# Two hybrid layers on one core: forget gates ahead of the queries, more low parts on GpSimd, other places for small steps

## The chip, the cores and the metric

The kernel runs on one core of a Trainium2 chip. The metric is the device time of one execution in microseconds (us); less is better. A core has five engines with a queue each: TensorE (PE; PEld is its weight load), VectorE (DVE), ScalarE (ACT), GpSimd (POOL) and SyncE (SP), which issues most transfers. PSUM is the memory that TensorE writes to, SBUF the memory for all else.

## The reference

A trunk of two layers over 512 tokens, with 16 meta tokens ahead of them (T = 528), width 1024, in float32. Each layer:

```python
xn = rmsnorm(h, attn_norm_g)
proj = xn @ w_in                       # fq, fk, fv, flog, rq, rk, rv, rg
logf = log_sigmoid(flog + b_fgate)     # 8 forget gates; c = cumsum(logf)
# 8 attention heads of 64: softmax(q.k / 8 + c[t] - c[s]) v, causal
# 4 retention heads of 128: rotary q and k, decay gamma_h^(t-s), chunks of 128
ret = head_groupnorm(ret) * silu(rg)
h = h + concat(fox_out, ret) @ w_out
hn = rmsnorm(h, ffn_norm_g)
h = h + (silu(hn @ w_gate) * (hn @ w_up)) @ w_down      # inner width 2816
```

At the end stands one more rmsnorm, and the 16 meta tokens are dropped.

## The kernel before, in words

Everything is held transposed: 128 channels on the partitions, the 528 tokens along the columns. A float32 product is made of three: each operand is split into a high part (hi) and the rest (lo), and hi x hi, w-hi x x-lo and w-lo x x-hi are summed in PSUM. So one *step* of a projection (one block of 128 x 128 weights) is six matmuls in layer 0, where the columns are cut in two halves of 264, and three where only the 512 real tokens are wanted (parts of layer 1). A *job* of `dense_steps` is eight steps with one weight tile `raw` of 128 x 1024. Its high part `whi` is cast by ScalarE (L199) and its low part `wlo` is subtracted (L202) by VectorE in pieces of 128 x 512 or, where the job's argument `pool` is set, by GpSimd in pieces of 128 x 128. `whi` and `wlo` have two buffers each; the next job's tile is converted at steps 1 and 4 of the job before.

PSUM is cut into two tiles of two banks (`psd`, results of the projections) and four of one bank (`psa`, all else), which go round in the order in which TensorE's steps ask for them.

The order on TensorE is written out by hand: a list `plan` of steps, into which `spread` and `ret_places` place the small steps (scores, transposes, sums of a norm) by their number among the steps of the projections. The order on the other engines is made by a scheduler from the same program; what stands in a `tc.high_priority()` block goes first, and what is pinned keeps its place.

What the change touches:
- `forget_sums`: the eight forget gates. z is scaled by the norm's R (L403), |z + b|, exp, ln on ScalarE, min(z + b, 0) (L407), a subtraction (L408) and a running sum (L409), then split into `fs` (L411, L412).
- `q_done`, `k_done`: the queries' and keys' projection leaves PSUM as `tq` (L442, L456), is split into `qo`/`qs` and `kc`/`kx`, and the forget sums are put below the keys in `kc` (L467). The first score (L519) reads `kc`.
- `out_proj` (`w_out`) and the first three gate and up blocks of `ffn` (plain blocks): which engine makes their low parts.
- The head norm of the retention: `col_rstd` lets TensorE sum the squares (L298, into psa), ScalarE take Ln (L303) and Exp (L304), and VectorE refine and scale (`nwt` L305, L307, L308, then `d` L792). `d` times the gate `sg` (silu, L418) is split into `mxh` and `mxl`, which the last steps of the output projection multiply. `ret_places(hd, ...)` sets the places of these steps; the ninth number is the head norm's.
- The tail: for the last token columns the squares of eight blocks are added by VectorE into `acc`, and the last ones summed apart on TensorE (L1164).

An `ACT_TABLE_LOAD` stands wherever ScalarE goes over from one family of functions to another, as between Exp and silu.

Of the kernel before, what the change touches and what calls it, by code (L numbers as in the profile page):

```python
# [39 lines left out]
def hybrid_kernel(ctx, tc, x_t, w_in, w_fl, w_out, w_gate, w_up, w_down, vecs, b_fg, rope, decay, mask, ident, out_t):  # L40
# [11 lines left out]

    idt = const.tile([128, 128], F32, name="idt")
    msk = const.tile([128, T], F32, name="msk")
    nc.vector.memset(msk[:, 0:T - 128], 0.0)
    pick = const.tile([32 + FH, FH], F32, name="pick")
    vec = const.tile([128, vecs.shape[1]], F32, name="vec")
    nc.scalar.dma_start(vec, vecs)
# [6 lines left out]
    nc.vector.memset(epsc, EPS)  # L65
    onec = const.tile([128, 1], F32, name="onec")
    nc.vector.memset(onec, 1.0)

    p_tiles, t_tiles, pm_tiles, v_tiles, end_tiles, q_tiles, k_tiles, f_tiles = [], [], [], [], [], [], [], []
    rot = {"pm": 0}  # L70
# [328 lines left out]
    def forget_sums(l, st):  # L399
        z = st["z"]  # L400
        z2 = tt("z2")[0:FH]
        with ExitStack() if l else tc.high_priority():
            nc.vector.scalar_tensor_tensor(z, z, RSC, st["R"][0:FH, :], ALU.mult, ALU.mult)  # L403
            nc.scalar.activation(z2, z, AF.Abs, bias=bfg[:, l:l + 1])
            nc.scalar.activation(z2, z2, AF.Exp, scale=-1.0)
            nc.scalar.activation(z2, z2, AF.Ln, bias=onec[0:FH])
        nc.vector.tensor_scalar(z, z, bfg[:, l:l + 1], 0.0, ALU.add, ALU.min)  # L407
        nc.vector.tensor_sub(z, z2, z)  # L408
        nc.vector.tensor_tensor_scan(z2, z, z, 0.0, ALU.add, ALU.max)  # L409
        with ExitStack() if l else tc.high_priority():  # L410
            nc.scalar.copy(f_tiles[0][0:FH], z2)  # L411
            nc.vector.tensor_sub(f_tiles[0][32:32 + FH], z2, f_tiles[0][0:FH].bitcast(F32))  # L412

# [19 lines left out]
    def fox_dense(l, g, ly, real, st):  # L433

        QC = REAL if real else FULL
        first = l + g == 0


        def q_done(ps):
            tq = tt("tq")  # L440
            with tc.high_priority() if first else ExitStack():
                nc.vector.scalar_tensor_tensor(sv(tq, real), pv(ps, real), RSC / 8.0, sv(ly["R"], real), ALU.mult, ALU.mult)  # L442
            st["q"] = []
            for s in range(2):
                t = at(f"qs{s}")
                a0, a1 = ROWS[s]
                b0, b1 = ROWS[1 - s]
                for o in (q_tiles[s], t):
                    nc.scalar.copy(sv(o, real, a0, a1), sv(tq, real, a0, a1))
                nc.vector.tensor_sub(sv(t, real, b0, b1), sv(tq, real, a0, a1), sv(q_tiles[s], real, a0, a1).bitcast(F32))  # L450
                st["q"].append((q_tiles[s], t))


        def k_done(ps):
            tk = tt("tq")
            nc.vector.scalar_tensor_tensor(sv(tk, False), pv(ps, False), RSC, sv(ly["R"], False), ALU.mult, ALU.mult)  # L456
            st["k"] = []
            for s in range(2):
                kc = k_tiles[s]
                kx = at(f"kx{s}")  # L460
                a0, a1 = ROWS[s]
                b0, b1 = ROWS[1 - s]
                nc.scalar.copy(kc[a0:a1, :], tk[a0:a1, :])
                nc.scalar.copy(kx[b0:b1, :], tk[a0:a1, :])
                nc.vector.tensor_sub(kx[a0:a1, :], tk[a0:a1, :], kc[a0:a1, :].bitcast(F32))
                hd = 2 * g + s
                (nc.gpsimd if g else nc.vector).tensor_scalar(kc[b0:b0 + 32 + FH, :], f_tiles[0].bitcast(F32), pick[:, hd:hd + 1], 0.0, ALU.mult, ALU.add)  # L467
                st["k"].append((kc, kx))

        def v_done(ps):  # L470
            vt = v_tiles[0]
            for t, (c0, c1) in zip(ps, FULL):
                nc.vector.scalar_tensor_tensor(vt[:, c0:c1], t[:, 0:c1 - c0], RSC, ly["R"][:, c0:c1],
                                               ALU.mult, ALU.mult)
            repeat(vt, SEQ, 1, SEQ + 32)
            if not real:
                repeat(vt, 0, 2, SEQ + 64)
            st["vt"] = vt

# [333 lines left out]
    def out_proj(l, rnd, mix, real):  # L813

        cols = REAL if real else FULL
        xs = lambda k: mix[k]["mix"]
        return sum([dense_steps(w_out[l, rnd, m2], [(4 * s, xs, 4, cols, add_h(2 * m2 + s, real)) for s in range(2)],
                                rnd == 0 or m2 < 2, rnd == 1 and m2 == 1) for m2 in range(NK // 2)], [])

    def ffn(l, st, real, last):  # L820
        QC = REAL if real else FULL
# [234 lines left out]
        for r, (f0, f1) in enumerate(ROUNDS):  # L1056
            for f in range(f0, f1):
                if f < PLAIN:
                    steps += dense_steps(w_gate[l, f], [(0, xs, NK, QC, g_done(f) if f else held.append)], banks=f == 1)
                    steps += dense_steps(w_up[l, f], [(0, xs, NK, QC, u_done(f))])  # L1060
                    continue
                u = Unit(f)
                steps += u.head()
                for v in tails:
                    v.last()
                    steps += v.tail()
                tails = []
                u.rest()
                steps += u.middle()
                if fills:  # L1070
                    p, g0, g1 = fills.pop(0)
                    j = down_job(p, g0, g1)
                    steps += down(j, 0, 2 * p, g0, g1, not real)
                    u.last()
                    steps += u.tail()
                    steps += down(j, 1, 2 * p + 1, g0, g1, False)
                else:
                    tails = [u]
            for p, g0, g1 in fills:
# [10 lines left out]
        else:  # L1090
# [34 lines left out]
            def square_b(m):  # L1125
                if m == 0:
                    t = fft("S", F32, (128, 6, w), 2)
                    fin["one"] = [t[:, i, 0:nb] for i in range(3)]
                    fin["acc"], fin["rb"], fin["tb"] = (t[:, i, 0:nb] for i in range(3, 6))
                    d = fin["acc"]  # L1130
                elif m < NK - 3:
                    fin["sq", m] = d = tt("sq")[:, 0:nb]
                else:
                    d = fin["one"][m - NK + 3]
                pin(nc.scalar.activation(d, h[m][:, cb], AF.Square))

            def sum_b(m):
# [78 lines left out]

            def after_7():
                square_b(7)
                v = psum_a()[:, 0:nb]
                sums(v, [fin["one"][0], fin["acc"]] + fin["one"][1:])  # L1220
                out_a(2)
                out_a(4)
                out_a(6)
                scale_b(3)
                root(fin["rb"], v)
                scale_b(4, 5, 6, 7)
                for i in range(3):
# [18 lines left out]
    def layer(l):  # L1246
# [66 lines left out]
        sums = [lambda: forget_sums(l, ly)]  # L1313
        plan = [lambda: enter_att(l), start]
        if l == 0:
            plan += [lambda: squares(ly, FULL, True, False)] + qk[:-2] + [first_parts] + gates + qk[-2:] + stats + [lambda: ly["wait"].pop(0)()] + sums + [lambda: ly["wait"].pop(0)()]
        else:
            plan += [lambda: squares(ly, FULL)] + q[:7] + stats + q[7:] + gates + sums + k
        plan += v + [ropes]
# [5 lines left out]

        for g in range(2):
            main, rest = fs[g]
            m0, r0, places = (((7 if l else 10.5, 31 if l else 32.5), (34, 40.5), (13, 33.5, 35.5, 37.5, 39, 40.5, 43, 44, 47.5, 48)),
                              ((0.5, 31.5), (32, 40), (13, 33.5, 35.5, 39.5, 39, 41.5, 43, 44, 47.5, 48)))[g]
            plan += merge(rd(g, "vqkg") + sum(fd(g + 1), []),  # L1330
                          spread(main, *m0), spread(rest, *r0), ret_places(g, *places))
# [6 lines left out]
        op = out_proj(l, 1, mixes[1], real)  # L1338
        base += op[0:3] + op[4:7] + op[8:11] + op[12:15]
        plan += merge(base, spread(main, 2, 46.5), spread(rest, 51, 56),  # L1340
                      ret_places(2, 26, 23.5, 24.5, 32, 28, 33.5, 36, 56.5, 40.5, 57.5),
                      ret_places(3, 52, 45.5, 47.5, 57.5, 55.5, 58.5, 60, 64.1, 63, 64.2))
        plan += [op[3], op[7], op[11], op[15]] + op[16:]
        up = ffn(l, ff, real, real)
        plan += [lambda: enter("ffn"), start_ffn] + up
# [78 lines left out]
```

## Time and profile before

| | before |
|---|---|
| median of three runs | 1271.29 us |
| the three runs | 1271.49, 1268.26, 1271.29 us |
| profiled execution | 1268.53 us, span 1266.7 us |
| TensorE busy | 1251.2 us (99%) |
| VectorE busy | 991.9 us (78%) |
| ScalarE busy | 704.8 us (56%) |
| GpSimd busy | 273.3 us (22%) |
| mean granted clock of TensorE | 0.997 |

The profile is of one execution; times in it count from the start of its span. A row of the timeline has the start, the duration, the engine, the line of the kernel, the operation, the tile written and the tiles read, the count, and in brackets how long the engine had been idle and who released it. Rows with a count above one give the time from the first start to the last end. Line numbers are those of the kernel before; after the change they move by a few (L442 becomes L440, L519 L524, L418 L416).

### The profile page before, as it was taken

To read this page: it belongs to the slowest core of one execution; us is meant where nothing else is said; L and a number is where in the kernel's file an instruction comes from. 1 tells how busy PE (TensorE), PEld (TensorE's weight loads), DVE (VectorE), ACT (ScalarE), POOL (GpSimd) and SP (SyncE) were. 2 spreads that over 40 slices of the span, in tenths; PEclk is the share of its full clock that TensorE was granted. 3 is DMA by queue.
4 is the path that set the end of the run, shared out by engine and by line. 5 is a ranking of instruction groups with operands and counts; after the bars stand their busy time and mean duration, and the time that the engine had idled before them with its cause. 6 is when DMAs were issued, how large, how long until landed. Compare 5 with 4: busy or idle time off the path is not lost.

```text
span 1266.7 us, 23526 instructions
## 1 busy us (share of the span) xinstructions
PE 1251.2 (99%) x9225; PEld 1194.1 (94%) x9225; DVE 991.9 (78%) x1804; ACT 704.8 (56%) x1301; POOL 273.3 (22%) x539
## 2 busy tenths in 40 slices
PE   9999999999999999999999999999999999999997
PEld 8899999999999999999999989998789999999996
DVE  8887756779988888887786877567899888888867
ACT  6766655676444444444466766557764444444445
POOL 3455546420000000000126556554100000000000
PEclk9999999999999999999999999999999999999999
DMA  6122222223333333332322122222223333333321
GB/s 218 50 76 75 76 77 72 72 67 118 104 97 100 100 101 100 101 101 84 101 77 84 60 86 74 70 90 67 100 94 123 100 101 101 100 101 101 100 84 67
DMA packets 43342, 116.19 MB, mean 92 GB/s; under 512 B 5088, under 2 KB 12000, under 8 KB 43232
## 3 DMA queue, kind: packets, MB, share of 16 engines
q1 hardware_dynamic: 42800, 114.41, 28.1%
q8 instruction: 72, 1.18, 0.4%
q14 instruction: 38, 0.31, 0.1%
q10 hardware_dynamic: 432, 0.29, 0.1%
HBM read 112.58 MB, written 2.10 MB: 91 GB/s over the span
## 4 chain that ended last, share of the span: by engine, by line
PE 93%; ACT 3%; DVE 3%; issue 1%; DMA 0%; ACTq 0%; DVEq 0%
PE psd L225 30%; PE psa L907 18%; PE psd L1042 14%; PE psd L907 13%; PE psa L225 5%; PE psa L1042 4%; PE psa L429 2%; PE psa L519 2%; PE psa L589 1%; PE psa L756 1%; PE psa L722 1%; ACT whi L199 1%; PE psa L298 0%; ACT xh L327 0%; DMA raw<-w_in 0%
## 5 line engine op out<-in xcount | busy, mean ns | idle before, releaser
L202 POOL TENSOR_TENSOR wlo<-raw,whi 128x128 fp32r<-128x128 f32 x504 | 258.2, 548 | 260.1 <-ACT whi L199 259.7
L225 PE MATMUL psd<-xh,whi 128*128 128x264 f32 (+1 forms) x792 | 195.5, 314 | 0.2 <-DVE tq L442 0.2
L225 PE MATMUL psd<-xl,whi 128*128 128x264 f32 (+1 forms) x792 | 186.7, 303 | 0.6 <-DVE xl L328 0.6
L225 PE MATMUL psd<-xh,wlo 128*128 128x264 f32 (+1 forms) x792 | 187.0, 304 | 0.0
L225 PEld LDWEIGHTS psd<-xh,whi 128*128 128x128 f32 x792 | 128.6, 189 | 5.0 <-issue 0.6
L225 PEld LDWEIGHTS psd<-xh,wlo 128*128 128x128 f32 x792 | 127.2, 188 | 6.2 <-DVE wlo L202 0.4
L225 PEld LDWEIGHTS psd<-xl,whi 128*128 128x128 f32 x792 | 127.8, 189 | 5.4 <-DVE xl L328 1.4
L199 ACT CAST whi<-raw 128x512 fp32r<-128x512 f32 (+1 forms) x168 | 97.9, 613 | 41.5 <-PE psd L225 28.4
L895 ACT CAST whi<-raw 128x1024 fp32r<-128x1024 f32 (+2 forms) x62 | 54.9, 885 | 51.3 <-PE psd L907 39.8
L895 ACT CAST fwhi<-raw 128x1024 fp32r<-128x1024 f32 (+2 forms) x62 | 55.6, 897 | 47.5 <-PE psd L907 40.0
L122 POOL MEMSET kc<- 64x528 f32 x2 | 1.1, 533 | 345.4 <-PE psa L907 345.4
L896 DVE TENSOR_TENSOR wlo<-raw,whi 128x1024 fp32r<-128x1024 f32 (+2 forms) x62 | 62.9, 1014 | 12.7 <-ACT whi L895 12.6
L896 DVE TENSOR_TENSOR fwlo<-raw,fwhi 128x1024 fp32r<-128x1024 f32 (+2 forms) x62 | 64.0, 1032 | 11.1 <-ACT fwhi L895 10.9
L907 PE MATMUL psa<-th,whi 128*128 128x264 f32 (+1 forms) x232 | 65.4, 282 | 0.0
L907 PE MATMUL psa<-th,wlo 128*128 128x264 f32 (+1 forms) x232 | 65.4, 282 | 0.0
L907 PE MATMUL psa<-tl,whi 128*128 128x264 f32 (+1 forms) x232 | 65.3, 282 | 0.0
L907 PE MATMUL psa<-th,fwhi 128*128 128x264 f32 (+1 forms) x224 | 63.4, 283 | 0.0
L907 PE MATMUL psa<-tl,fwhi 128*128 128x264 f32 (+1 forms) x224 | 63.3, 283 | 0.0
L907 PE MATMUL psa<-th,fwlo 128*128 128x264 f32 (+1 forms) x224 | 63.2, 282 | 0.0
L536 ACT ACTIVATE pr<-pr,nmax 128x144 f32<-128x144 f32 (+1 forms) x64 | 36.8, 576 | 45.4 <-DVE nmax L523 26.1
L895 ACT CAST fwhi<-S 128x1024 fp32r<-128x1024 f32 x20 | 21.0, 1049 | 68.6 <-PE psa L907 66.5
L973 ACT COPY e<-psa 128x264 f32<-128x264 f32 (+1 forms) x114 | 42.8, 376 | 28.4 <-PE psa L907 24.1
(365 smaller groups left out, 4041.2 us busy)
## 6 DMA issues: line engine op xcount, KB each, us to landing
raw<-w_in SPq DMA_DIRECT2D x54, 512.0 KB, 3.5
raw<-w_gate SPq DMA_DIRECT2D x44, 512.0 KB, 3.9
fraw<-w_up SPq DMA_DIRECT2D x38, 512.0 KB, 3.5
raw<-w_down SPq DMA_DIRECT2D x64, 256.0 KB, 2.9
raw<-w_out SPq DMA_DIRECT2D x16, 512.0 KB, 3.4
raw<-w_down SPq DMA_DIRECT2D x32, 192.0 KB, 2.5
raw<-w_up SPq DMA_DIRECT2D x6, 512.0 KB, 3.5
h<-x_t SPq DMA_DIRECT2D x8, 264.0 KB, 4.5
```

The source lines that it names most:

```text
L199: pin(nc.scalar.copy(hi, job["raw"][:, c0:c1]), pinned)
L202: pin(sub(lo[:, c:c + step], job["raw"][:, c0 + c:c0 + c + step], hi[:, c:c + step].bitcast(F32)), pinned)
L225: nc.tensor.matmul(ps[1][b][:, 0:c1 - c0], w[:, wk, :], x[:, c0:c1], start=(k == 0 and i == 0), stop=(k == n - 1 and i == 2))
L429: nc.tensor.transpose(ps[:, 128 * j:128 * j + 128], src[:, o:o + 128], idt)
L519: nc.tensor.matmul(sc[0:nq, 0:c1 - c0], qq[:, q0:q0 + nq], kk[:, c0:c1], start=(i == 0), stop=(i == 1))
L536: nc.scalar.activation(pr, pr, AF.Exp, bias=nmax[0:nq], scale=-1.0, accum_out=rsum)
L589: nc.tensor.matmul(po[:, c0:SEQ], v[:, j, :], pp[:, j, META + c0:T], start=(j == 0 and i == 0), stop=(j == 4))
L895: nc.scalar.copy(hi, src)
L896: nc.vector.tensor_sub(lo, src, hi.bitcast(F32))
L907: nc.tensor.matmul(bank()[:, 0:b.shape[-1]], a[:, o + k, :], b, start=(fresh and k == 0 and i == 0), stop=(k == n - 1 and i == 2), skip_gr ...
L973: nc.scalar.copy(self.t["e"][:, i], self.t["x"][:, 0:w])
L1042: nc.tensor.matmul(v[:, 0:c1 - c0], a[:, s * n + k, :], b[:, c0:c1], start=(k == 0 and i == 0), stop=(k == n - 1 and i == 2))
```

## The change

`forget_sums` runs whole at high priority in layer 0, and all of it stands ahead of the queries in the plan; the subtraction is done in the running sum. In the first pair of heads the second `kc` goes to ScalarE, the first stays on VectorE at high priority. The first clearing of `msk` goes to GpSimd. GpSimd makes the low parts of all jobs of `out_proj` and of the plain gate and up blocks. In the tail two squares instead of three are kept apart. Places move: head 0 of the retention 10.5 to 11 and 37.5 to 38, head 2's norm 40.5 to 49, head 3's 60 to 60.6 and 63 to 63.6.

```diff
-    nc.vector.memset(msk[:, 0:T - 128], 0.0)
...
+    nc.gpsimd.memset(msk[:, 0:T - 128], 0.0)
...
             nc.scalar.activation(z2, z2, AF.Ln, bias=onec[0:FH])
-        nc.vector.tensor_scalar(z, z, bfg[:, l:l + 1], 0.0, ALU.add, ALU.min)
-        nc.vector.tensor_sub(z, z2, z)
-        nc.vector.tensor_tensor_scan(z2, z, z, 0.0, ALU.add, ALU.max)
-        with ExitStack() if l else tc.high_priority():
+            nc.vector.tensor_scalar(z, z, bfg[:, l:l + 1], 0.0, ALU.add, ALU.min)
+            nc.vector.tensor_tensor_scan(z2, z2, z, 0.0, ALU.add, ALU.subtract)
             nc.scalar.copy(f_tiles[0][0:FH], z2)
             nc.vector.tensor_sub(f_tiles[0][32:32 + FH], z2, f_tiles[0][0:FH].bitcast(F32))
...
-                (nc.gpsimd if g else nc.vector).tensor_scalar(kc[b0:b0 + 32 + FH, :], f_tiles[0].bitcast(F32), pick[:, hd:hd + 1], 0.0, ALU.mult, ALU.add)
+                own, of = kc[b0:b0 + 32 + FH, :], f_tiles[0].bitcast(F32)
+                if g:
+                    nc.gpsimd.tensor_scalar(own, of, pick[:, hd:hd + 1], 0.0, ALU.mult, ALU.add)
+                elif s:
+                    nc.scalar.activation(own, of, AF.Copy, scale=pick[:, hd:hd + 1])
+                else:
+                    with tc.high_priority():
+                        nc.vector.tensor_scalar(own, of, pick[:, hd:hd + 1], 0.0, ALU.mult, ALU.add)
...
         return sum([dense_steps(w_out[l, rnd, m2], [(4 * s, xs, 4, cols, add_h(2 * m2 + s, real)) for s in range(2)],
-                                rnd == 0 or m2 < 2, rnd == 1 and m2 == 1) for m2 in range(NK // 2)], [])
+                                True, rnd == 1 and m2 == 1) for m2 in range(NK // 2)], [])
...
-                    steps += dense_steps(w_gate[l, f], [(0, xs, NK, QC, g_done(f) if f else held.append)], banks=f == 1)
-                    steps += dense_steps(w_up[l, f], [(0, xs, NK, QC, u_done(f))])
+                    steps += dense_steps(w_gate[l, f], [(0, xs, NK, QC, g_done(f) if f else held.append)], True, banks=f == 1)
+                    steps += dense_steps(w_up[l, f], [(0, xs, NK, QC, u_done(f))], True)
...
             def after_7():
                 square_b(7)
+                sum_b(5)
                 v = psum_a()[:, 0:nb]
-                sums(v, [fin["one"][0], fin["acc"]] + fin["one"][1:])
+                sums(v, [fin["one"][0], fin["acc"], fin["one"][1]])
...
-            plan += [lambda: squares(ly, FULL, True, False)] + qk[:-2] + [first_parts] + gates + qk[-2:] + stats + [lambda: ly["wait"].pop(0)()] + sums + [lambda: ly["wait"].pop(0)()]
+            plan += [lambda: squares(ly, FULL, True, False)] + qk[:-2] + [first_parts] + gates + qk[-2:] + stats + sums + [lambda: ly["wait"].pop(0)()] * 2
...
-                      ret_places(2, 26, 23.5, 24.5, 32, 28, 33.5, 36, 56.5, 40.5, 57.5),
-                      ret_places(3, 52, 45.5, 47.5, 57.5, 55.5, 58.5, 60, 64.1, 63, 64.2))
+                      ret_places(2, 26, 23.5, 24.5, 32, 28, 33.5, 36, 56.5, 49, 57.5),
+                      ret_places(3, 52, 45.5, 47.5, 57.5, 55.5, 58.5, 60.6, 64.1, 63.6, 64.2))
```

On VectorE at the start of layer 0, right behind the norm's R, stood before (`tq` from psd is first the queries', then the keys'; `z` are the forget gates, `cr` the rotary table that is scaled by R):

```order
L308 SCALAR_TENSOR_TENSOR R<-nwt,R 128x528
L442 SCALAR_TENSOR_TENSOR tq<-psd,R 128x528
L403 SCALAR_TENSOR_TENSOR z<-z,R 8x528
L1258 SCALAR_TENSOR_TENSOR cr<-cr,R 128x528
L450 TENSOR_TENSOR qs_427<-tq,qo_103 64x528
L456 SCALAR_TENSOR_TENSOR tq<-psd,R 128x528
```

and on the same engine at the same place stands now:

```order
L308 SCALAR_TENSOR_TENSOR R<-nwt,R 128x528
L403 SCALAR_TENSOR_TENSOR z<-z,R 8x528
L1264 SCALAR_TENSOR_TENSOR cr<-cr,R 128x528
L440 SCALAR_TENSOR_TENSOR tq<-psd,R 128x528
L407 TENSOR_SCALAR z<-z,bfg 8x528
L454 SCALAR_TENSOR_TENSOR tq<-psd,R 128x528
```

The queries' `tq` has moved behind the scaling of the gates and of `cr`.

On ScalarE at head 3 of the retention in layer 0, between the squares of the head's output (`sqh`) and the high part of its gated output (`mxh`), stood before:

```order
L769 ACTIVATE sqh<-d 128x528
L303 ACTIVATE r<-psa,epsc 128x264 x2
L199 CAST whi<-raw 128x512
L304 ACTIVATE r<-r 128x528
L418 ACT_TABLE_LOAD
L418 ACTIVATE sg<-sg 128x528
L420 ACT_TABLE_LOAD
L199 CAST whi<-raw 128x512
L150 CAST mxh_3866<-d 128x528
```

and now:

```order
L774 ACTIVATE sqh<-d 128x528
L199 CAST whi<-raw 128x512 x2
L303 ACTIVATE r<-psa,epsc 128x264 x2
L416 ACT_TABLE_LOAD
L416 ACTIVATE sg<-sg 128x528
L304 ACT_TABLE_LOAD
L304 ACTIVATE r<-r 128x528
L418 ACT_TABLE_LOAD
L150 CAST mxh_3865<-d 128x528
```

Exp (L304) has moved behind the silu (L416), with a table load more, and both weight casts stand ahead of Ln (L303). Layer 1 has the same order there.

On VectorE at head 2 in layer 0, where the norm's chain (L305, L307, L308) stood ahead of the last attention score of that place (the two ISA rows of 128x264), it stood before:

```order
L305 TENSOR_TENSOR nwt<-r 128x528
L151 TENSOR_TENSOR rkl<-tq,rkh 128x528
L593 TENSOR_TENSOR mixt<-psa,ol 64x512
L307 SCALAR_TENSOR_TENSOR nwt<-psa,nwt 128x264 x2
L523 ISA pr,nmax<-psa,msk 128x264
L523 ISA nmax 128x1
```

and it stands now some twenty rows later, among the operations that read the transposes (`pth`/`ptl` the attention weights, `mean` and `sq` the values):

```order
L305 TENSOR_TENSOR nwt<-r 128x528
L151 TENSOR_TENSOR ptl<-psa,pth 128x2x128
L307 SCALAR_TENSOR_TENSOR nwt<-psa,nwt 128x264
L690 TENSOR_REDUCE mean<-psa 128x4
L690 TENSOR_REDUCE mean<-psa 128x1
L691 SCALAR_TENSOR_TENSOR sq<-mean,psa 128x512
L691 SCALAR_TENSOR_TENSOR sq<-mean,psa 128x128
L307 SCALAR_TENSOR_TENSOR nwt<-psa,nwt 128x264
L151 TENSOR_TENSOR ptl<-psa,pth 128x3x128
```

The two L307, which release the two psa buffers of the norm, have moved from between `mixt` and a score to either side of the values' reduces. On TensorE the norm's matmuls (L298) now stand two steps ahead of the transposes of `pr` (128x128 x2), then `pd` (x5) and `pr` (x3).

On GpSimd the run of 96 pieces of `wlo` at the end of each layer's projections becomes one of 160; VectorE has the sixteen rows of 128x512 fewer that made them.

More of the change, by code (lines that the diff above doesn't have):

```diff
@@ L1127, in square_b @@
                     t = fft("S", F32, (128, 6, w), 2)
-                    fin["one"] = [t[:, i, 0:nb] for i in range(3)]
+                    fin["one"] = [t[:, i, 0:nb] for i in range(2)]
                     fin["acc"], fin["rb"], fin["tb"] = (t[:, i, 0:nb] for i in range(3, 6))
                     d = fin["acc"]
-                elif m < NK - 3:
+                elif m < NK - 2:
                     fin["sq", m] = d = tt("sq")[:, 0:nb]
                 else:
-                    d = fin["one"][m - NK + 3]
+                    d = fin["one"][m - NK + 2]
                 pin(nc.scalar.activation(d, h[m][:, cb], AF.Square))
@@ L1327, in layer @@
             main, rest = fs[g]
-            m0, r0, places = (((7 if l else 10.5, 31 if l else 32.5), (34, 40.5), (13, 33.5, 35.5, 37.5, 39, 40.5, 43, 44, 47.5, 48)),
+            m0, r0, places = (((7 if l else 11, 31 if l else 32.5), (34, 40.5), (13, 33.5, 35.5, 38, 39, 40.5, 43, 44, 47.5, 48)),
                               ((0.5, 31.5), (32, 40), (13, 33.5, 35.5, 39.5, 39, 41.5, 43, 44, 47.5, 48)))[g]
```

## Prediction

> **What bounds the kernel now.** I read the page first, then the waits of TensorE, then the stretches around the longest of them. The profiled run took 1268.53 us; its span is
>
> ```profile
> span 1266.7 us, 23526 instructions
> ```
>
> so 1.8 us lie outside the span. TensorE works nearly without a break. Its waits (what waited, for whom; sum, times, longest, in us) are these:
>
> ```profile
> PE psa L519 <- DVE kc L467: 3.1, 1, 3.1
> PE psa L1277 <- DVE wide L63: 2.0, 1, 2.0
> PE psa L519 <- DVE mixt L593: 0.7, 1, 0.7
> PE psa L756 <- DVE rsl L151: 0.7, 2, 0.4
> PE psd L225 <- DVE xl L328: 0.6, 2, 0.4
> PE psd L225 <- DVE tq L442: 0.2, 1, 0.2
> PE psa L1164 <- ACT S L1135: 0.2, 1, 0.2
> ```
>
> Together 7.5 us, 2.0 of them at the start before any data is there. The other engines work beside it, so the time changes only by a wait of TensorE that goes or comes, or by its clock. The change adds or removes no matmul of a projection. All that is worth costing is therefore: which of these seven rows go, and which new ones come.
>
> The longest wait has a second cost. The view of stretches gives, for each, its length, the busy time of TensorE, of its weight loads, VectorE, ScalarE and GpSimd, and then the granted clock:
>
> ```profile
> 38.27:41.68 3.41, 1.07 (x11) 1.10 (x11) 2.85 (x7) 0.85 (x5) 3.41 (x7) 1.00 0.00 0
> 41.68:45.08 3.40, 3.40 (x19) 3.40 (x17) 1.63 (x7) 1.29 (x6) 0.53 (x2) 0.50 0.42 149
> 245.42:249.73 4.31, 4.31 (x39) 4.31 (x38) 4.26 (x10) 2.14 (x6) 4.31 (x8) 1.00 0.00 0
> 1256.80:1260.20 3.40, 1.89 (x8) 1.44 (x8) 3.20 (x7) 2.78 (x9) 0.00 (x0) 1.00 0.49 166
> ```
>
> After a stretch in which TensorE was busy for 1.07 of 3.41 us (31%) the next 3.40 us ran at half clock. Half of 3.40 was lost: 1.7 us. The last row, 56% busy at 1.00, stands in the tail, and there I use only that 56% is a share that a stretch can have at full clock.
>
> **The change, part by part.** Start. The row
>
> ```profile
> 0.89 0.39 DVE L55 MEMSET msk<- 128x400 f32 x1 [0.89 <-PEq L1412]
> ```
>
> leaves VectorE for GpSimd, so all that VectorE does up to the first matmul is 0.39 earlier: **-0.4** (0 to -0.5).
>
> New wait for the first query. VectorE's rows after the norm's R are
>
> ```profile
> 27.50 0.88 DVE L308 SCALAR_TENSOR_TENSOR R<-nwt,R 128x528 f32<-128x528 f32 x1
> 28.49 0.71 DVE L442 SCALAR_TENSOR_TENSOR tq<-psd,R 128x528 f32<-128x528 f32 x1
> 29.11 0.98 DVE L403 SCALAR_TENSOR_TENSOR z<-z,R 8x528 f32<-8x528 f32 x1
> 30.03 0.69 DVE L1258 SCALAR_TENSOR_TENSOR cr<-cr,R 128x528 f32<-128x528 f32 x1
> ```
>
> and TensorE already waited 0.2 for that tq, which empties a bank pair of psd. Now z and cr stand ahead of it. By the starts z holds VectorE for 0.92 (29.11 to 30.03), cr for about 0.6 as tq did (28.49 to 29.11): the matmuls behind tq wait 1.5 longer, **+1.5** (1.0 to 1.9).
>
> The wait for kc goes. Before, the first kc was written late:
>
> ```profile
> 39.80 1.26 DVE L467 TENSOR_SCALAR kc<-fs,pick 40x528 fp32r<-40x528 f32 x2
> ```
>
> The first of the two ended near 40.4, so TensorE, 3.1 late, had arrived at 37.3. After the change the subtraction, a second kx, sr and pd no longer stand ahead of kc; at the 0.6 to 0.7 that such operations take above this is 2.5, kc is there at about 37.3, or 37.9 if z costs more, and TensorE comes at 37.3 + 1.5 - 0.4 = 38.4. **-3.1**. The second kc goes to ScalarE, which I cost at nothing, since a later score reads it. With the idle time the half clock goes: **-1.7**, if no new wait of 1.5 to 1.9 makes its own stretch idle enough (1.9 of 3.41 leaves 44%, between the 31% that did it and the 56% above). [...] What follows on TensorE gains 1.6 on VectorE, which still has to release the banks of the values' transposes: **+0.5** (0 to 1.2).
>
> Small orders. The mixt wait (head 2's norm no longer stands between) goes, **-0.7**; the two rsl waits go, since rsh and rsl are now ahead of the state's parts, **-0.7**; the larger xl wait, 0.4, goes because VectorE lost low parts to GpSimd, **-0.4**.
>
> Head 3 of the retention. This is the part that speaks against the change. In layer 0 before, ScalarE, then VectorE, then the matmul that needs the outcome were:
>
> ```profile
> 263.07 0.85 ACT L303 ACTIVATE r<-psa,epsc 128x264 f32<-128x264 f32 x2 [1.41 <-PE psa L298]
> 263.81 0.62 ACT L199 CAST whi<-raw 128x512 fp32r<-128x512 f32 x1
> 264.32 0.65 ACT L304 ACTIVATE r<-r 128x528 f32<-128x528 f32 x1
> 264.99 1.28 ACT L418 ACT_TABLE_LOAD   x1
> 266.29 0.65 ACT L418 ACTIVATE sg<-sg 128x528 f32<-128x528 f32 x1
> ...
> 269.16 0.64 ACT L150 CAST mxh<-d 128x528 fp32r<-128x528 f32 x1 [0.30 <-DVE d L785]
> ```
>
> ```profile
> 265.01 0.95 DVE L305 TENSOR_TENSOR nwt<-r 128x528 f32<-128x528 f32 x1 [0.38 <-ACT r L304]
> 265.99 0.77 DVE L307 SCALAR_TENSOR_TENSOR nwt<-psa,nwt 128x264 f32<-128x264 f32 x2
> 266.80 0.71 DVE L308 SCALAR_TENSOR_TENSOR r<-nwt,r 128x528 f32<-128x528 f32 x1
> 267.54 0.77 DVE L792 SCALAR_TENSOR_TENSOR d<-d,gn,r 128x528 f32<-128x528 f32 x1
> 268.42 0.71 DVE L785 TENSOR_TENSOR d<-d,sg 128x528 f32<-128x528 f32 x1
> ```
>
> ```profile
> 272.41 0.41 PE L225 MATMUL psd<-mxh,whi 128*128 128x264 f32 x2
> ```
>
> Now two casts, Ln, a table load, the silu and a further table load stand ahead of Exp. The casts can begin when the last step before the output projection is done, near 263.3: 2 x 0.55 + 0.8 + 1.28 + 0.65 + 1.28 + 0.65 puts the end of Exp at 269.0, where it was 264.97. The chain nwt to d took 265.01 to 269.13, 4.1: d is ready at 273.1, mxh at 273.8, mxl 0.7 later. TensorE wants mxh at 272.41 and mxl one matmul pair later: a wait of 1.4, then 0.5, together 1.9; nothing is left that could be put ahead of these steps, as all other parts of the projection wait for them or for the banks they hold. I take 1.8 in each layer, since layer 1 works on 512 columns: **+3.6** (2 to 4.5).
>
> Head 2. Its norm's matmuls (L298) move from ahead of the last attention score to just ahead of the transposes. They hold two of the four psa buffers until L307 has read them. TensorE, ScalarE and VectorE before, at this place in layer 0:
>
> ```profile
> 247.68 0.71 PE L429 MATMUL psa<-idt,pd 128*128 128x128 f32 x5
> 248.14 0.49 PE L225 MATMUL psd<-xh,whi 128*128 128x264 f32 x2
> 248.47 0.41 PE L225 MATMUL psd<-xl,whi 128*128 128x264 f32 x2
> 248.71 0.41 PE L225 MATMUL psd<-xh,wlo 128*128 128x264 f32 x2
> 248.96 0.49 PE L429 MATMUL psa<-idt,pr 128*128 128x128 f32 x3
> ```
>
> ```profile
> 246.42 0.52 ACT L150 CAST rsh<-sd 128x400 fp32r<-128x400 f32 x1
> ```
>
> ```profile
> 248.46 0.88 DVE L685 TENSOR_REDUCE mean<-psa 128x4 f32<-128x512 f32 x2
> 249.25 0.87 DVE L686 SCALAR_TENSOR_TENSOR sq<-mean,psa 128x512 f32<-128x512 f32 x2
> ```
>
> The buffers go round, so the fifth pd transpose (near 248.1) takes the buffer of the first norm half, the pr transposes (248.96) that of the second. Ln now stands behind the cast of rsh, which I put at 246.1 to 246.9: Ln 0.8, Exp 0.65, nwt 0.7 to 0.95, one L307 0.4 give 248.7 to 249.7 for the first half, a wait of 0.6 to 1.6. The second L307 stands behind two L690 and two L691 (0.88 and 0.87): 1.9 to 2.1 later, against 0.9 between the two wants: 1.0 more. I take the lower end, as VectorE has lost the chain that it did here before: **+1.7** (0.8 to 2.6) in layer 0. Layer 1 has one buffer for 512 columns and its L307 stands ahead of the reduces; but VectorE has no gap left up to its last ptl there, so I take **+1.0** (0 to 1.5).
>
> Low parts on GpSimd. Sixteen weight tiles more go there, eight pieces each; what GpSimd needs is shown by
>
> ```profile
> 245.42 4.31 POOL L202 TENSOR_TENSOR wlo<-raw,whi 128x128 fp32r<-128x128 f32 x8 [6.03 <-ACT whi L199]
> ```
>
> 4.31 for eight pieces, 0.54 each, while VectorE was 99% busy (4.26 of 4.31, in the row of that stretch). A tile's matmuls are eight steps of three pairs 0.24 apart, 5.8 (248.47 to 248.71 is one pair): GpSimd keeps ahead by 1.5 a tile, which hides it. **0**; without that cover it costs what a piece exceeds 0.73. In the tail one square fewer is summed apart, but the wait of 0.2 for S remains with a later square first: **+0.2** (0 to 0.5).
>
> The sum: -0.4 + 1.5 - 3.1 - 1.7 + 0.5 - 0.7 - 0.7 - 0.4 + 3.6 + 1.7 + 1.0 + 0.2 = +1.5. On the profiled run's 1268.53 this is 1270.0. That run lies with the lowest of the three shown (1268.26 to 1271.49; median 1271.29), so on the median 1270.0 is a tenth of a per cent down, on the profiled run a tenth up.
>
> **Rivals.** *Faster: the new waits at heads 2 and 3 do not come.* For it: before, mxh was done 2.6 ahead of its matmul, and VectorE, relieved by low parts, may shorten the chain (its nwt took 0.95 where a similar operation takes 0.7). Against: two table loads of 1.28 and a silu in front of Exp are fixed. Without the 6.3 it is 1263.7; without half of them 1266.9.
>
> *Slower: the clock falls at the new waits.* Places: the wait for the first query and the op steps of head 3 in both layers, with 1.8, 1.9 and 1.8 idle, and the two waits of head 2 in layer 0, 1.7 within 2.6. Each leaves 44 to 50% of a stretch of 3.4 busy if it lies in one stretch. It decides if the bound is above that share, and costs 1.7 each time, as at 41.68. Two of four: +3.4, 1273.4; three: 1275.1; four: 1276.8.
>
> *Slower: GpSimd is held up by VectorE in the plain blocks.* There VectorE works almost without pause. If each piece waited for half of a VectorE operation of 0.7, it took 0.9, a tile 7.2 against 5.8, and 16 tiles 22 us: 1292. The point is 0.73 a piece. The eight pieces in 4.31 beside a full VectorE speak against it. [...]
>
> *No trace of it: gains and new waits cancel to under 1 us.* This lies inside my forecast.
>
> **How the numbers follow.** A measurement of this kernel can tell about 0.3%, 3.8 us, from no change. Forecast 1270.0, with the bounds of the terms adding to some 3.5 either way: chance 0.46. Faster rival 0.28, reaching 1263.7. Clock rival 0.18, of which half is beyond 1275. GpSimd rival 0.08. Range 1263.5 to 1275.5: it leaves out GpSimd's case and the far part of the clock's. Taken against the median, where 1267.5 is the edge of faster and 1275.1 that of slower, and with some of the forecast's own width beyond both: faster 0.30, same 0.42, slower 0.28.
>
> **What would show it.** Right: no wait at L524 for kc, clock 1.00 from 41 to 45; waits of about 1.8 for tq near 29, for mxh and mxl near 272 and at the same step of layer 1, and for L307 at the transposes near 248. In ScalarE's rows of head 3, three table loads around silu and Exp. Wrong: no wait of TensorE at the op steps; a clock row of 0.50 behind any of the new waits; a row that waits for wlo of GpSimd in the FFN.

## The result, and the profile after

The changed kernel takes 1286.51 us (median of four runs, 1286.20 to 1286.67) against 1270.37 (four runs, 1268.26 to 1271.49): ratio 1.0129, 95% interval 1.0111 to 1.0146. It is 16 us slower, outside the range. The profiled execution took 1286.20 us. Of its page, the span, TensorE's busy time, and GpSimd's:

```profile
span 1284.3 us, 23641 instructions
...
PE 1257.0 (98%) x9223; PEld 1195.2 (93%) x9223; DVE 990.5 (77%) x1768; ACT 708.8 (55%) x1305; POOL 357.8 (28%) x668
```

TensorE's waits after the change (what waited, for whom; sum, times, longest):

```profile
PE psd L225 <- DVE sg L848: 5.1, 2, 2.8
PE psd L225 <- ACT whi L199: 3.1, 2, 2.6
PE psa L594 <- DVE ptl L151: 1.8, 3, 0.8
PE psd L225 <- DVE tq L440: 1.7, 1, 1.7
PE psd L225 <- ACT mxh L150: 1.6, 2, 1.0
PE psa L1283 <- DVE wide L62: 1.6, 1, 1.6
PE psa L1169 <- ACT S L1140: 0.9, 1, 0.9
PE psa L727 <- DVE ptl L151: 0.7, 1, 0.7
PE psd L225 <- DVE h L815: 0.6, 1, 0.6
PE psd L225 <- DVE mxl L151: 0.5, 2, 0.2
```

The waits for kc, mixt and xl are gone. The two largest are new and lie in the plain blocks: `sg` is the first gate's result, which VectorE can write only when the norm's R is there, and while it waits the psd tile is held. In layer 0 the clock fell to 0.50 behind both, from 310.6 and from 327.7 (the first of them, by stretch: length, busy time of TensorE, its loads, VectorE, ScalarE, GpSimd, granted clock):

```profile
310.60:314.00 3.40, 3.40 (x16) 3.40 (x17) 2.34 (x4) 1.54 (x3) 1.39 (x3) 0.50 0.21 64
```

The waits sum to 19.2 us against 7.5 (the rows left out have 0.2 to 0.4 each). The half clock took one stretch before the tail and takes two now, 1.7 more. That is 13.4 of the 17.6 by which the span grew. The rest lies within TensorE's busy time, which grew from 1251.2 to 1257.0 (1.7 of that is the half clock); what made it longer these views do not resolve.

Why sg came late shows in VectorE's operations by shape, before (273 to 305 us) and after (273 to 312), the columns being count, busy time, mean ns:

```profile
L328 DVE SCALAR_TENSOR_TENSOR xl<-h,vec,xh 128x528 fp32r<-128x528 f32 x8 | 5.8, 759 | 0.0
L348 DVE TENSOR_TENSOR ss<-ss,sq 128x528 f32<-128x528 f32 x7 | 4.9, 698 | 0.0
L151 DVE TENSOR_TENSOR tl<-S,th 128x1056 fp32r<-128x1056 f32 x2 | 2.5, 1256 | 0.0
...
L871 DVE SCALAR_TENSOR_TENSOR S<-h,vec,S 128x264 f32<-128x264 f32 x4 | 1.8, 482 | 0.0
...
L843 DVE SCALAR_TENSOR_TENSOR sg<-psd,R 128x528 f32<-128x528 f32 x1 | 0.7, 699 | 0.0
```

```profile
L328 DVE SCALAR_TENSOR_TENSOR xl<-h,vec,xh 128x528 fp32r<-128x528 f32 x8 | 6.9, 874 | 1.3 <-ACT xh L327 1.3
L348 DVE TENSOR_TENSOR ss<-ss,sq 128x528 f32<-128x528 f32 x7 | 6.4, 910 | 0.1
L876 DVE SCALAR_TENSOR_TENSOR S<-h,vec,S 128x264 f32<-128x264 f32 x8 | 5.2, 664 | 0.0
L151 DVE TENSOR_TENSOR tl<-S,th 128x1056 fp32r<-128x1056 f32 x3 | 4.5, 1501 | 0.0
...
L848 DVE SCALAR_TENSOR_TENSOR sg<-psd,R 128x528 f32<-128x528 f32 x1 | 0.7, 695 | 0.0
```

Of these operations those with two operands in SBUF became 0.12 to 0.25 us longer in the mean (482 to 664 ns for 264 columns, 759 to 874 and 698 to 910 for 528, 1256 to 1501 for 1056); the one with an operand in PSUM (sg) did not (699 and 695). Beside them GpSimd worked through 32 pieces in a row:

```profile
276.42 21.98 POOL L202 TENSOR_TENSOR wlo<-raw,whi 128x128 fp32r<-128x128 f32 x32 [9.04 <-ACT whi L199]
```

That is 0.69 a piece, where 0.54 was seen before.

The wait for whi came about in another way. GpSimd's pieces hold `raw`, the tile of weights as loaded, until they have read it. Here they ended at 322.17, and the load that needed the tile was issued at 322.20. ScalarE stood waiting for what it brought, with the cast of whi next in its queue:

```profile
318.63 3.54 POOL L202 TENSOR_TENSOR wlo<-raw,whi 128x128 fp32r<-128x128 f32 x4 [1.83 <-ACT whi L199]
322.20 0.81 SPq L1027 DMA_DIRECT2D raw<-w_down  x2
325.16 0.83 ACT L900 CAST fwhi<-raw 128x768 fp32r<-128x768 f32 x1 [4.58 <-DMA raw<-w_down]
326.56 0.51 PE L225 MATMUL psd<-xh,whi 128*128 128x264 f32 x2 [2.59 <-ACT whi L199]
```

So here GpSimd was late itself (3.54 for four pieces).

Also, the scheduler had put work for later blocks (S eight times instead of four, tl three instead of two) ahead of the chain to R. So two causes are possible: GpSimd's reads, or the order.

### The profile page after: what moved, and what is told of

The parts are those of the page before. It is cut to its first block, busy times and chain, and to the rows that moved or that the text cites. A ratio compares the mean times of both kernels' runs of the same rounds, so it can differ in the third digit from the quotient of the medians.

```text
span 1284.3 us, 23641 instructions
## 1 busy us (share of the span) xinstructions
PE 1257.0 (98%) x9223; PEld 1195.2 (93%) x9223; DVE 990.5 (77%) x1768; ACT 708.8 (55%) x1305; POOL 357.8 (28%) x668
## 4 chain that ended last, share of the span: by engine, by line
PE 85%; DVE 9%; ACT 4%; issue 1%; POOL 1%; DMA 0%; DVEq 0%; SPq 0%; ACTq 0%; POOLq 0%
PE psd L225 25%; PE psa L912 18%; PE psd L1047 14%; PE psd L912 13%; PE psa L1047 4%; PE psa L225 3%; PE psa L427 2%; PE psa L594 1%; PE psa L524 1%; PE psa L761 1%; ACT whi L199 1%; PE psa L727 1%; DVE ss L348 1%; PE psa L389 1%; DVE xl L328 1%
## 5 line engine op out<-in xcount | busy, mean ns | idle before, releaser
L202 POOL TENSOR_TENSOR wlo<-raw,whi 128x128 fp32r<-128x128 f32 x632 | 342.6, 578 | 287.2 <-ACT whi L199 266.0
L225 PE MATMUL psd<-xh,whi 128*128 128x264 f32 (+1 forms) x792 | 197.2, 317 | 10.5 <-DVE sg L848 5.1
L900 ACT CAST fwhi<-raw 128x1024 fp32r<-128x1024 f32 (+2 forms) x62 | 55.6, 897 | 52.9 <-PE psd L912 39.5
L900 ACT CAST whi<-raw 128x1024 fp32r<-128x1024 f32 (+2 forms) x62 | 54.8, 885 | 50.8 <-PE psd L912 41.2
L900 ACT CAST fwhi<-S 128x1024 fp32r<-128x1024 f32 x20 | 21.0, 1049 | 68.3 <-PE psa L912 66.5
L978 ACT COPY e<-psa 128x264 f32<-128x264 f32 (+1 forms) x114 | 42.9, 376 | 27.4 <-PE psa L912 23.2
```

The lines of the kernel that those rows point to most:

```text
L202: pin(sub(lo[:, c:c + step], job["raw"][:, c0 + c:c0 + c + step], hi[:, c:c + step].bitcast(F32)), pinned)
L225: nc.tensor.matmul(ps[1][b][:, 0:c1 - c0], w[:, wk, :], x[:, c0:c1], start=(k == 0 and i == 0), stop=(k == n - 1 and i == 2))
L900: nc.scalar.copy(hi, src)
L978: nc.scalar.copy(self.t["e"][:, i], self.t["x"][:, 0:w])
```

## The experiments

Times are medians beside runs of the kernel before on the same chip, ratios with their 95% intervals.

**Which part of the change.** Four kernels; first the low parts of projection and plain blocks both back on VectorE:

```diff
-                                True, rnd == 1 and m2 == 1) for m2 in range(NK // 2)], [])
+                                rnd == 0 or m2 < 2, rnd == 1 and m2 == 1) for m2 in range(NK // 2)], [])
...
-                    steps += dense_steps(w_up[l, f], [(0, xs, NK, QC, u_done(f))], True)
+                    steps += dense_steps(w_up[l, f], [(0, xs, NK, QC, u_done(f))])
```

(and the same for w_gate).

> The changed kernel with the low parts of the last projection jobs and of the plain blocks back on VectorE, all else as changed. Contention (GpSimd pieces and VectorE operations with two SBUF operands slow one another, so the chain to R and sg comes late): the waits for sg (5.1 us) and whi (3.1) and the two stretches at half clock (3.4) go, 1286.5 falls to 1271 to 1275. Order (the chain is late because of the row order that the other parts of the change gave): 1283 to 1287, the sg waits stay.

Measured: 1272.92 against 1270.66, ratio 1.0018 (1.0009 to 1.0027). The waits for sg and whi are gone.

The kernel before with only these lines changed, the other way round:

> The kernel before with only these low parts moved to GpSimd. Contention: 1270.4 rises by 11 to 14, to 1281 to 1285, with waits for sg near 305 and 930 and VectorE's subtractions of 528 columns at 0.95 instead of 0.70. Order: within 2 us of before.

Measured: 1284.65, ratio 1.0107 (1.0089 to 1.0125). The same two waits appear:

```profile
PE psd L225 <- DVE sg L843: 5.1, 2, 2.8
PE psa L519 <- DVE kc L467: 3.1, 1, 3.1
PE psd L225 <- ACT whi L199: 2.6, 1, 2.6
```

The changed kernel with the plain blocks' lines back, and then with the projection's line back:

> The changed kernel with the low parts of the plain gate and up blocks alone back on VectorE, those of the projection still on GpSimd. If the backlog on VectorE is built in the plain blocks: 1273 to 1277. If it is built by the projection's pieces already (GpSimd works on 32 pieces from 276 to 298 without pause): 1282 to 1286, sg waits stay.

> The changed kernel with the low parts of the last projection jobs alone back on VectorE, those of the plain blocks still on GpSimd. Backlog from the plain blocks: 1282 to 1286. Backlog from the projection's pieces: 1273 to 1277.

Measured: 1271.56, ratio 1.0011 (1.0002 to 1.0021), and 1290.16, ratio 1.0152 (1.0137 to 1.0167). The first lies 1.4 below and the second 4.2 above the range that was expected for the plain blocks; the side is theirs in both, and the other theory is far off. It is the plain blocks. The projection's low parts seem to do better on GpSimd: 1271.56 against 1272.92 without them, and 1286.51 (from the first runs) against 1290.16.

**Reads or order.** The kernel before, with work added: behind each low part of the plain blocks GpSimd subtracts, for nothing,

```diff
+            if job["pool"] == 2:
+                for c in range(c1 - c0):
+                    pin(nc.gpsimd.tensor_sub(scr, hi[:, c].bitcast(F32), idt), pinned)
```

> The kernel before, all low parts where they were; in the plain blocks GpSimd makes eight more subtractions a tile, of whi and a constant, into a tile that nobody reads (work added, not moved). Contention: VectorE keeps its own low parts and its operations with two SBUF operands rise from 0.70 to 0.95 there, so slower than with the low parts moved or about as slow: 1280 to 1292. Late low parts or buffers held by GpSimd (nothing here waits for the new pieces but the release of whi): 1270 to 1273.

Measured: 1285.62, ratio 1.0123 (1.0109 to 1.0136). The order on VectorE and ScalarE is that of before, row for row. TensorE waits for VectorE's results:

```profile
PE psd L229 <- DVE xl L332: 4.4, 5, 1.2
PE psd L229 <- DVE sg L847: 4.1, 2, 2.3
```

The same with pieces that write and hardly read:

```diff
+                    pin(nc.gpsimd.tensor_sub(scr[:, 0:1], hi[:, c, 0:1].bitcast(F32), idt[:, 0:1]), pinned)
+                    pin(nc.gpsimd.memset(scr, 0.0), pinned)
```

> The kernel before with work added on GpSimd in the plain blocks as in the run with dummy reads, but each piece reads one column only (128x1, to tie it to the tile) and then clears 128x400, so it writes and hardly reads. If it is GpSimd's reading of SBUF that slows VectorE's operations with two SBUF operands: these stay near 0.70 and the time within 2 us of before. If any GpSimd operation beside VectorE does it: they rise to about 0.95 and the time to 1278 to 1288.

Measured: 1292.54, ratio 1.0172 (1.0158 to 1.0186), so each theory missed: of the first the operations came out and the time did not, of the second neither. VectorE's operations, by shape, with reads (first two rows) and with memsets (last two):

```profile
L332 DVE SCALAR_TENSOR_TENSOR xl<-h,vec,xh 128x528 fp32r<-128x528 f32 x8 | 7.0, 900 | 0.0
...
L352 DVE TENSOR_TENSOR ss<-ss,sq 128x528 f32<-128x528 f32 x7 | 5.9, 840 | 0.0
```

```profile
L333 DVE SCALAR_TENSOR_TENSOR xl<-h,vec,xh 128x528 fp32r<-128x528 f32 x8 | 5.9, 764 | 0.0
L353 DVE TENSOR_TENSOR ss<-ss,sq 128x528 f32<-128x528 f32 x7 | 4.9, 702 | 0.0
```

Beside memsets they keep their 0.76 and 0.70. But now some of GpSimd's one-column reads are long:

```profile
292.26 2.61 POOL L206 TENSOR_TENSOR scr<-whi,idt 128x1 f32<-128x1 f32 x1
...
295.44 0.19 POOL L206 TENSOR_TENSOR scr<-whi,idt 128x1 f32<-128x1 f32 x1
```

They take 0.19 to 2.61, 0.49 in the mean of 96; what makes some of them long was not shown. They read whi, GpSimd falls behind, and ScalarE can't write the next whi until they are through:

```profile
325.73 1.04 ACT L900 CAST whi<-raw 128x1024 fp32r<-128x1024 f32 x1 [4.11 <-POOL scr L206]
```

The profile has TensorE wait 1.8 for the next whi (L900) in each layer and 3.2 and 3.0 for e (L978). So the time of this run is not the slowing of VectorE but, as the profile reads, the buffers that a late GpSimd holds: a second way in which GpSimd's work costs time.

The order alone: the changed kernel, with GpSimd clearing the plain blocks' low parts instead of subtracting them:

```diff
+                if job["pool"] == 3:
+                    pin(nc.gpsimd.memset(lo[:, c:c + step].bitcast(F32), 0.0), pinned)
+                    continue
```

> The changed kernel, but in the plain blocks GpSimd clears the low parts instead of subtracting them (the low parts of the plain weights are left out of the sum), so that it writes and does not read. VectorE and ScalarE keep the changed kernel's order there but for one swapped pair. If the order on VectorE (work for later blocks ahead of the chain to R and sg) costs by itself: waits for sg of 1 to 3 stay, 1277 to 1284. If it takes GpSimd's reads: no wait for sg over 0.5, 1271 to 1274, as with the plain low parts back on VectorE (1271.6).

Measured: 1271.58 against 1270.70, ratio 1.0009 (0.9999 to 1.0019). No wait for sg is left, and between 287 and 312 us, where GpSimd only clears, VectorE's operations have their old lengths (664, 1501 and 920 ns in the same stretch of the changed kernel):

```profile
L151 DVE TENSOR_TENSOR tl<-S,th 128x1056 fp32r<-128x1056 f32 x4 | 5.0, 1248 | 0.0
L879 DVE SCALAR_TENSOR_TENSOR S<-h,vec,S 128x264 f32<-128x264 f32 x8 | 3.7, 484 | 0.0
...
L351 DVE TENSOR_TENSOR ss<-ss,sq 128x528 f32<-128x528 f32 x3 | 2.1, 699 | 0.0
```

So the new order costs nothing by itself; the 15 us of the plain blocks take GpSimd's reads. In the run with dummy reads GpSimd holds up the loads no more than before (they wait 2.3 us for it between 270 and 345 us, as in the kernel before; in the changed kernel 38), so the slowing of VectorE is enough for a loss of that size. How the 15 us of the changed kernel divide between the slower VectorE and the `raw` that GpSimd holds was not separated: clearing the low parts takes away both.

Half of the plain tiles (up on GpSimd, gate on VectorE):

> The changed kernel with the low parts of the three plain gate tiles back on VectorE, those of the three up tiles still on GpSimd. With all six back it was 1271.6, with none 1286.5. If the cost grows with the number of pieces: 1278 to 1280. If it has a threshold (the chain to R must end before TensorE needs a psd tile): near 1272 or near 1286.

Measured: 1286.94, ratio 1.0131 (1.0117 to 1.0145): as much as with all. The wait for sg shrank to 1.6, but VectorE, which keeps the gates' low parts and still runs beside GpSimd, is late elsewhere. This is near one of the two values expected for a threshold, but the threshold named, the chain to R and sg, is not what kept the time up:

```profile
PE psa L912 <- DVE wlo L901: 3.5, 1, 3.5
PE psd L225 <- DVE wlo L202: 2.1, 1, 2.1
```

**The rest of the change.** In the changed kernel one operation of VectorE, the lower bound `ge` of the retention's gate, took 3.47 us, beside a run of eight pieces; in the profile of before it took 0.53, also beside such a run (the first row is after, then GpSimd's run beside it, then before):

```profile
63.01 3.47 DVE L664 TENSOR_SCALAR ge<-sg 128x528 f32<-128x528 f32 x1
```

```profile
62.79 3.39 POOL L202 TENSOR_TENSOR wlo<-raw,whi 128x128 fp32r<-128x128 f32 x8
```

```profile
65.49 0.53 DVE L659 TENSOR_SCALAR ge<-sg 128x528 f32<-128x528 f32 x1
```

Written with two operands:

```diff
-            nc.vector.tensor_scalar_max(u, x, -80.0)
+            nc.vector.scalar_tensor_tensor(u, x, -80.0, x, ALU.max, ALU.max)
```

> The kernel before with one operation of VectorE (the lower bound of the gate, ge from sg, both in SBUF) written with two SBUF operands in place of one and a number; same values. In the profiles this operation took 0.53 us in one execution of before and 3.0 to 3.5 in five others of five kernels, next to a run of eight GpSimd pieces. Theory, it is shut out for the whole run of pieces and its late end causes the waits of TensorE near 58 to 74: the runs of before that lie near 1271 come down, median 1267.5 to 1269, spread under 1.5, no ge operation over 1 us. Rival, the spread of before has another cause: median 1270 to 1271.5, spread as before (some 4).

Measured: 1271.31, ratio 1.0007 (0.9998 to 1.0016). No gain: with two operands it still took 3.3 us and more in the next two kernels, which have this line too; what it took in this kernel is not known.

> The operation of the run before this with two operands, and of the change only the forget gates (forget_sums, kc, the order in the plan). By the steps of the prediction: -3.1 for kc, -1.7 for the clock, +1.5 for tq, so 3 below the kernel with the ge operation alone. Rival, what follows (values' transposes, psa) eats it: within 1 of it.

Measured: 1267.61, ratio 0.9971 (0.9961 to 0.9980), 3.7 below the kernel with the ge line alone. The edit is the diff of `forget_sums`, `k_done` and the plan.

> The ge operation with two operands, and of the change only the places of the small steps. From the profile of the changed kernel: waits for mxh and mxl at head 3 (0.9 and 1.2 in the two layers), at head 2 (0.7 and 1.0) against mixt (0.7) and rsl (0.7) gone: 2 to 3 above the kernel with the ge operation alone. Rival, the places gain: 1 below it.

Measured: 1275.93, ratio 1.0046 (1.0034 to 1.0059), 4.6 above the ge line alone: more than expected. Of that, by the profile, the waits at heads 2 and 3 are 1.3 for ptl, 1.6 for mxh, 0.5 for mxl and 0.4 in small ones, less 0.7 for mixt and 0.4 for one rsl, 2.7 together as expected. The profile also has 2.5 of waits between 62 and 75 us, behind a ge of 3.72; whether the kernel with the ge line alone has as much is not known, so the rest stays open.

`ge` made by GpSimd (`nc.gpsimd.tensor_scalar_max`), in the kernel before, then with the parts that gained, then with tq first, then in the changed kernel:

> The kernel before with the lower bound ge of the gates made by GpSimd, in its queue between the pieces, instead of VectorE. With two SBUF operands on VectorE it still took 3.3 to 3.7 us in three profiles, so the operand count is not what shuts it out. Theory, any such operation that starts within a run of pieces can be held to the run's end, and that makes the runs of before near 1271: median 1267.5 to 1269. Rival, the spread has another cause: 1270 to 1271.5.

Measured: 1275.56, ratio 1.0035 (1.0021 to 1.0049). That misses both ranges. In layer 0 there is no wait near 66 to 74 but one of 0.17; in layer 1 ScalarE stands in its queue until GpSimd's ge is there, and TensorE waits for rsh:

```profile
706.12 0.79 PE L756 MATMUL psa<-rsh,rvh 128*128 128x512 f32 x1 [3.18 <-ACT rsh L150]
```

> The kernel before with what gained so far: forget gates as changed, msk on GpSimd, low parts of the last projection jobs on GpSimd (those of the plain blocks stay on VectorE, places as before), and ge on GpSimd. If the parts add: forget -3.0, projection -1.4, ge -2 (if its theory holds): 1264 to 1266, and no slower than 1267.6 if only the first holds.

> The same with the queries' tq ahead of z and cr again (plan order of before; sums within the running sum and kc as changed). The wait for tq falls from 1.75 to about 0.3, kc may come up to 0.7 late: 0 to 1.5 below the run before this. Rival, a wait for kc of over 1.5 comes back and the half clock with it: 1 to 3 above.

> The changed kernel with ge made by GpSimd. Its waits from 66 to 71 (0.66, 0.44, 0.20, 0.25, together 1.55) follow a ge operation of 3.47 us. If that is their cause they go: 1284 to 1285.5. If not: 1286 to 1287.

Measured: 1269.52, ratio 0.9994 (0.9985 to 1.0003); 1270.36, ratio 0.9999 (0.9990 to 1.0007); 1289.07, ratio 1.0144 (1.0130 to 1.0158). All three missed, and all three have the wait of 2.9 for rsh in layer 1. With tq first the wait for kc is 1.43 and that for tq 0.48: together no less than the 1.76 that they replace.

Last, the parts that gained with ge left on VectorE, and with ge on GpSimd in layer 0 alone (`nc.vector if l else nc.gpsimd`):

> The kernel before with the forget gates as changed, msk on GpSimd and the last projection's low parts on GpSimd; ge stays on VectorE. If the projection's 1.4 (the difference of two runs of the changed kernel) adds to the forget gates' 3.0: 1265.5 to 1267. If not: 1267 to 1269.

> The same with ge made by GpSimd in layer 0 alone. With GpSimd in both layers the waits near 66 to 74 went (from 1.5 to 0.17) but in layer 1 a wait of 3 for rsh came. If both are as the profiles say: 1 to 1.5 below the run before this, and no wait for rsh in layer 1.

Measured: 1268.05, ratio 0.9980 (0.9970 to 0.9990), so the projection's part did not add to the forget gates' here; and 1264.91, ratio 0.9956 (0.9944 to 0.9969), the fastest of all, 5.6 us below before and 3.1 below the run before this, where 1 to 1.5 was expected. In the two profiles 1.55 of waits between 67 and 72 us are gone, and so is a stretch at half clock behind the wait for tq, worth 1.7. The wait itself is still there, so that part is owed to where it lay (see the last section) and not to ge. The largest waits left:

```profile
PE psd L225 <- DVE tq L440: 1.7, 1, 1.7
PE psa L1282 <- DVE wide L62: 1.6, 1, 1.6
```

## Why the prediction was wrong

**The step that failed** is "Low parts on GpSimd: 0". It measured 14 to 15 us: 1286.51 with, 1271.56 to 1272.92 without. The working asked only whether GpSimd keeps ahead of TensorE. In the mean it did (0.69 a piece over 32, under the 0.73 named), if not for every tile (6.47 us for the eight pieces at 298.89, 0.81 each), and TensorE waited 0.2 in all for its wlo. It did not ask what GpSimd's reads do to VectorE, which was busy 31.52 of 32.00 us there and whose chain to sg had little to spare (sg began at 303.82; TensorE needed its tile at 305.14). The row taken as evidence (eight pieces in 4.31 us beside a full VectorE) comes from a stretch where most of VectorE's operations read PSUM or are small; the price stood in that same stretch and went unread: a subtraction rsl of 528 columns took 0.91 us at 245.96 where it takes 0.71 at 69.77. In the plain blocks most operations have two SBUF operands. Nor did it ask what waits for the buffers that GpSimd holds while it reads: the load of w_down, and behind it the wait of 2.59 for whi.

**The GpSimd rival**, given 0.08, named the right place and direction and half of the path: it priced late pieces, 1292. TensorE's first wait was for VectorE, which the rival left out; the second goes back to GpSimd's late pieces. The eight pieces in 4.31 us, which the prediction set against it, did not carry over: the 32 pieces from 276.42 took 0.69 each and the eight behind them 0.81, instead of 0.54. On VectorE's side the sum ss of 528 columns took 698 ns before, 910 in the changed kernel, 840 beside dummy reads and 702 beside memsets. How the one engine makes the other slower was not shown, and the ge operation (last section) lost far more than these.

**The other terms** sum to +1.5; without the plain blocks' low parts the kernel is 0.9 above before (1271.56 against 1270.66) and 2.3 without the projection's too. Single ones, predicted and measured in the profile: start -0.4, measured 2.02 to 1.59; tq +1.5, measured 0.25 to 1.74; kc -3.1 and the clock -1.7, both gone (alone, the forget gates gave -3.7 against -3.3 for these three terms); mixt -0.7 and xl -0.4, gone; rsl -0.7, gone in layer 1 but 0.25 came in layer 0. Head 3 came as described but smaller: 0.63 + 0.23 and 1.00 + 0.22 us instead of 1.8 a layer. ScalarE did what the order said, and Exp ended where predicted:

```profile
264.33 0.84 ACT L303 ACTIVATE r<-psa,epsc 128x264 f32<-128x264 f32 x2
265.19 1.28 ACT L416 ACT_TABLE_LOAD   x1
...
267.15 1.28 ACT L304 ACT_TABLE_LOAD   x1
268.44 0.65 ACT L304 ACTIVATE r<-r 128x528 f32<-128x528 f32 x1
```

TensorE came 0.6 later, and from the end of Exp to mxh it took 3.87 (269.09 to 272.96) where 4.1 was taken. Head 2 in layer 0 was 0.20 and 0.51 instead of 1.7, in layer 1 1.0 (0.22 and 0.77) as predicted; but the waits are for ptl and rkl, and none is for L307, for which the prediction had TensorE wait, so the agreement in layer 1 is luck. Not foreseen: 1.55 of waits near 66 to 71 behind the 3.47 us ge, 0.56 for ptl at 58.73, 0.6 for h at 289.61, and 0.9 instead of 0.4 for S in the tail. The bounds named for the terms add to 4.8 down and 4.1 up, not to 3.5; wider by that much, the range would still not have reached 1286.

**The clock rival** was right that the clock would fall behind new waits, but in another place: it fell behind the two waits of 2.84 and 2.59. Behind the wait of 1.74 for tq it stayed at 1.00 here; in two later runs it fell behind the same wait, so that the -1.7 came out whole was luck in part.

## What to carry to other kernels

Before work is moved to GpSimd, look at what VectorE does in that stretch: where its operations have two SBUF operands, price GpSimd's reads at 0.12 to 0.25 us on each of them, as measured here (ge lost 2.5 to 3.2), and ask who waits for VectorE there, and for the buffers that GpSimd holds while it reads, not only whether GpSimd's results are in time. A stretch used as evidence must have the same mix of operations as the place of the change. Moving half of the work kept the whole loss.

## What the runs showed of the hardware

- One VectorE operation took about as long as the run of GpSimd pieces beside it (3.47 and 3.39 us in the changed kernel), but not in every trace: the first ge of layer 0, of 528 columns, took 0.53 us in two profiles (before, and the run with dummy reads) and 3.05 to 3.72 in eleven others, with one SBUF operand and with two. What decides it is open; it began some 0.2 us after the run's first piece in both the short and the long case (65.49 after 65.27; 63.01 after 62.79). With it moved off VectorE in layer 0 the runs spread over 1.1 us (1264.53 to 1265.63, five runs) where the same kernel with ge on VectorE spread over 2.0 (1266.62 to 1268.60, nine) and before over 3.7; that ge makes the levels of before was not shown.
- In these traces the clock's fall followed not the length of a wait, but how much of one stretch of a grid of 3.41 us the wait left busy. In each of the twelve traces that have several, the changes of the granted clock stand whole multiples of 3.41 us from one another (the falls of the changed kernel at 310.62 and 327.69 stand five of them apart). On the grid that they give, a wait of 1.74 for tq in the changed kernel lay across two stretches and one of 1.76 in the run with forget gates, projection and ge on GpSimd lay in one:

```profile
27.32:30.73 3.41, 2.06 (x17) 1.84 (x16) 3.34 (x6) 0.93 (x2) 3.41 (x6) 1.00 0.47 154
30.73:34.15 3.42, 3.03 (x25) 3.06 (x26) 3.36 (x6) 3.38 (x7) 1.39 (x3) 1.00 0.29 48
```

```profile
27.66:31.07 3.41, 1.65 (x14) 1.47 (x13) 3.36 (x6) 1.57 (x3) 3.41 (x5) 1.00 0.38 139
31.07:34.48 3.41, 3.41 (x17) 3.41 (x17) 3.32 (x6) 3.37 (x7) 0.75 (x2) 0.50 0.43 136
```

The first left 2.06 us busy and the clock stayed; the second left 1.65 and it fell. Likewise a wait of 2.89 for rsh, in one stretch (0.52 busy), brought a fall in the latter run, and one of 2.88 in the run with tq first, over two (1.75 and 1.98 busy), did not; nor did 3.47 for wlo in the run with half the plain tiles (1.63 and 1.71). Over all 18 traces of executions between 1265 and 1290 us (where there is one change alone, the grid is laid by it), all 26 falls ahead of the tail came behind a stretch with at most 1.65 of 3.41 us busy, and every stretch with less than 1.62 brought one; between the two both happened. So the bound that the prediction left between 31% and 56% is near 48% here, and where the grid lies, which differs from trace to trace, decided whether a wait of some 1.8 to 3.5 us (estimated from these shares) cost a further 1.7. This may be part of the spread of all these kernels; that was not tested.
